# First MLP product of a hybrid encoder block turned token-major, with a seven-product scheme for a quarter of its K pairs

## The chip, the cores and the metric

The kernel runs on one core of one Trainium2 chip. The metric is the device time of one execution, in microseconds (us). A second number, the span of the profiled execution, runs from its first instruction to its last. Engines are called as in the profile: PE is TensorE's matmuls, PEld its weight loads, DVE is VectorE, ACT is ScalarE, POOL is GpSimd, and SP is the engine that only issues DMAs here.

## The reference

One layer of a streaming encoder on 256 tokens with model width 2048, in float32. `n = RMSNorm(h)`, an input projection, two groups of heads (gated DeltaNet and HGRN2), an output projection, and then a squared-ReLU MLP:

```
h = h + concat(y_A, y_B) @ W_out
n = rms_norm(h, norm_ffn_w)
h = h + square(relu(n @ w1)) @ w2        # w1: 2048 x 8192, w2: 8192 x 2048
out = rms_norm(h, norm_final_w)
```

The change touches `n @ w1` and what stands next to it. The RMS factor of a token's row commutes with ReLU and with the squaring, so the kernel leaves it out of `n` and multiplies the row by its square (`fs[:, 6 + hf]`, line 765) only after `@ w2`.

## The kernel before, in words

**Precision.** The matmuls take a rounded float32 form (`F32R`). To keep float32 accuracy each operand is split in two, `hi` (rounded, by ACT, line 117) and `lo = w - hi` (by DVE, line 118), and a product is `hi*hi + lo*hi + hi*lo`, three matmuls into one accumulator. Weights arrive as float32 tiles of 128 x 2048 (1 MB, one DMA on SP's queue, three buffers) and are split in pieces of 128 x 1024, with three buffers for `hi` and three for `lo`.

**Stages, in order of time.** The input projection with the heads' own work between (to 447 us); the output projection (447 to 550 us, lines 652 to 679); the first MLP product (550 to 913 us, lines 698 to 715); the second MLP product (913 us to the end, lines 718 to 756) with the final norm.

**Output projection (line 664).** Token-major: the stationary operand is 128 x 128 of y transposed (`yT`), the moving operand 128 x 512 of the split weight. The sum goes to `h`, 128 tokens to a half, two halves (`hf`). After each half of the columns, `h` is transposed by PE in 128 x 128 blocks (line 678) into `hT`, which ACT and DVE scale by the norm weight and split (`to_T`, lines 164 to 167).

**First MLP product.** Feature-major: the stationary operand is a 128 x 128 block of the weight, the moving one is `hT`. Line 709 takes `hi` of the weight against 512 columns (256 tokens of `hi`, 256 of `lo`), line 710 `lo` of the weight against the 256 `hi` tokens. For each of 64 blocks of 128 features and each of 16 K blocks there is one such pair, 1024 pairs in all. Four feature blocks share four PSUM banks (`acc` or `accb`, in turn). Lines 713 to 715 add the two halves of a bank and write `relu(x)*x`, feature-major, into `g`.

**Second MLP product (`ff2`, line 731).** Token-major: stationary is 128 x 128 of the split `g` (`gs`), moving 128 x 512 of the split weight. Three matmuls for each of 64 K blocks, two token halves and four groups of 512 columns, 1536 in all (the last of them in two halves of 256 columns).

**Order of work.** The program is written in the order above, and a planner that simulates the engines orders each engine's queue: what is ready goes first, and an instruction's place in the source is its priority. The two transposes at a time that stand between matmuls of the next half in the profile come from that. On the chip each queue keeps the planned order.

Of the kernel before, what the change touches and what calls it, by code (L numbers as in the profile page):

```python
# [73 lines left out]
def hybrid_block(ctx: ExitStack, tc: tile.TileContext, x, xt, w_in, w_ab, params, w_out, w_ff1, w_ff2,  # L74
                 norm_final_w, consts, out):
    nc = tc.nc
    PE, ACT, DVE, POOL, SP = nc.tensor, nc.scalar, nc.vector, nc.gpsimd, nc.sync
# [24 lines left out]
    def acc_a():  # L102
        return psA.tile([P, 512], F32, tag="acc", name="acc")
# [37 lines left out]
    for a, b in zip(xs, ws):  # L141
        SP.dma_start(*a)
        SP.dma_start(*b)
    SP.dma_start(cst, consts)
    wab = mp.tile([P, KT, 16], F32, tag="Xt", name="wab")
    SP.dma_start(wab, w_ab)

    def C(name):
        a, b = _CONST_COLS[name]
        return cst[:, a:b]  # L150

    ident, ones = C("ident"), C("ones")
    eps = C("eps")
# [487 lines left out]
    def acc_b():  # L641
        return psB.tile([P, 512], F32, tag="accb", name="accb")

    hT = bpool.tile([P, KT, 2 * T], F32R, tag="xT", name="hT")
    h = bpool.tile([P, 2 * D], F32, tag="h", name="h").rearrange("p (f c) -> p f c", f=2)
# [5 lines left out]
    fs = cpool.tile([P, 16], F32, tag="fs", name="fs")  # L651
    for nh in range(2):
        accs = [acc_a() for _ in range(4)]
        for kp in range(8):
            w = wtile()
            SP.dma_start(w, w_out[nh * 8 + kp])
            for kk in range(2):
                k = 2 * kp + kk
                hi, lo = split(w[:, kk * 1024:(kk + 1) * 1024], 1024)
                for hf in range(2):  # L660
                    for a, ww in ((0, hi), (T, hi), (0, lo)):
                        st = yT(k, a + hf * P, a + hf * P + P)
                        for c in range(2):
                            PE.matmul(accs[2 * hf + c], lhsT=st, rhs=ww[:, c * 512:(c + 1) * 512],  # L664
                                      start=(k == 0 and a == 0 and ww is hi), stop=(k == 2 * NH - 1 and ww is lo))
        for hf in range(2):
            for c in range(2):
                hv = h[:, hf, nh * 1024 + c * 512:nh * 1024 + (c + 1) * 512]
                DVE.tensor_tensor(out=hv, in0=accs[2 * hf + c], in1=hv, op=ALU.add)
            hv = h[:, hf, nh * 1024:(nh + 1) * 1024]  # L670
            ACT.activation(sqj, hv, AF.Square, accum_out=fs[:, 2 * hf + nh:2 * hf + nh + 1])
        for k2 in range(4):
            pt = acc_b()
            for kk in range(2):
                k = nh * 8 + k2 * 2 + kk
                ptk = pt[:, kk * T:(kk + 1) * T]
                for hf in range(2):
                    PE.transpose(ptk[:, hf * P:(hf + 1) * P], h[:, hf, k * P:(k + 1) * P], ident)
                to_T(hT, k, ptk, cols[:, 16 + k:17 + k])
    for hf in range(2):  # L680
        DVE.tensor_tensor(out=fs[:, 4 + hf:5 + hf], in0=fs[:, 2 * hf:2 * hf + 1], in1=fs[:, 2 * hf + 1:2 * hf + 2],
                          op=ALU.add)
# [11 lines left out]
    def g(f):
        return gt[f // NG][:, f % NG, :]

    nfw = fp.tile([P, D], F32, tag="nfw", name="nfw")
    for fg in range(NF // 4):
        accs = [acc_a() if fg % 2 == 0 else acc_b() for _ in range(4)]
        for kq in range(4):  # L700
            w = wtile()
            SP.dma_start(w, w_ff1[fg * 4 + kq])
            for q in range(2):
                hi, lo = split(w[:, q * 1024:(q + 1) * 1024], 1024)
                for kk in range(2):
                    k = 4 * kq + 2 * q + kk
                    for f in range(4):
                        cs = slice(kk * 512 + f * P, kk * 512 + (f + 1) * P)
                        PE.matmul(accs[f], lhsT=hi[:, cs], rhs=hT[:, k, :], start=(k == 0), stop=False)  # L709
                        PE.matmul(accs[f][:, T:], lhsT=lo[:, cs], rhs=hT[:, k, 0:T], start=False, stop=(k == KT - 1))  # L710
        for f in range(4):
            lot = fp.tile([P, T], F32, tag="lotf", name="lotf", bufs=2)
            ACT.copy(lot, accs[f][:, T:])
            DVE.tensor_tensor(out=lot, in0=accs[f][:, 0:T], in1=lot, op=ALU.add)
            DVE.scalar_tensor_tensor(out=g(4 * fg + f), in0=lot, scalar=0.0, in1=lot, op0=ALU.max, op1=ALU.mult)
    SP.dma_start(nfw, norm_final_w.unsqueeze(0).to_broadcast([P, D]))

    accs = [[acc_a() for _ in range(4)], [acc_b() for _ in range(4)]]
    TAIL = 3
    held = []  # L720

# [10 lines left out]
                      start=(first and a == 0 and ww is hi), stop=(last and ww is lo))  # L732

    keep = None
    for f in range(NF):
        w = wtile()
        SP.dma_start(w, w_ff2[f])
        gs = fp.tile([P, 2 * T], F32R, tag="gs", name="gs", bufs=4)
        split(g(f), None, gs[:, 0:T], gs[:, T:])
        n = f - (NF - TAIL)  # L740
        if n == 0:
            keep = fp.tile([P, TAIL - 1, 2, D], F32R, tag="g0", name="keep")
        hl = []
# [13 lines left out]
    fin = fp.tile([P, 12], F32, tag="fin", name="fin")  # L757
    sqf = fp.tile([P, 512], F32, tag="sqf", name="sqf")
    o = fp.tile([P, 2, D], F32, tag="o", name="o", bufs=1)
    NP = 5  # L760
    DVE.memset(fin, 0.0)

    def piece(hf, n, a, b, acc):
        hv = h[:, hf, a:b]
        DVE.scalar_tensor_tensor(out=hv, in0=acc, scalar=fs[:, 6 + hf:7 + hf], in1=hv, op0=ALU.mult, op1=ALU.add)
        ACT.activation(sqf[:, 0:b - a], hv, AF.Square, accum_out=fin[:, hf * NP + n:hf * NP + n + 1])
        DVE.scalar_tensor_tensor(out=o[:, hf, a:b], in0=hv, scalar=float(D) ** 0.5, in1=nfw[:, a:b], op0=ALU.mult,
                                 op1=ALU.mult)

    def row_rstd(hf, n, last):  # L770
# [11 lines left out]

    def scaled(hf, eng, a, b, s):
        if eng is ACT:
            ACT.activation(h[:, hf, a:b], o[:, hf, a:b], AF.Copy, scale=s)
        else:
            DVE.tensor_scalar(h[:, hf, a:b], o[:, hf, a:b], s, None, ALU.mult)
        (ACT if eng is ACT else SP).dma_start(out[0, hf * P:(hf + 1) * P, a:b], h[:, hf, a:b])

    hv = h[:, 1, 1536:2048]  # L790
# [27 lines left out]
def _laid_out(i):  # L818
# [5 lines left out]
    for base in (0, 4112):  # L824
        v = w[:, base:base + 4096].reshape(2, 8, P, 2, 2, NH, P)
        groups.append(v.transpose(5, 3, 0, 2, 1, 4, 6).reshape(4 * NH, P, 2048))

    def columns(a):
        return a.reshape(-1, P).T

# [9 lines left out]
        "w_ff1": i["w_ff1"][0].reshape(4, 4, P, 16, 512).transpose(3, 0, 2, 1, 4).reshape(64, P, 2048),  # L840
# [24 lines left out]
```

## Time and profile before

| | |
|---|---|
| median of 3 runs (range) | 1270.77 us (1270.59 to 1271.01) |
| the profiled execution's own time | 1271.04 us |
| its span | 1269.3 us |
| PE busy | 1239.6 us, 98% of the span |
| DVE busy | 855.0 us, 67% |
| ACT busy | 673.9 us, 53% |
| DMA | 229.65 MB, mean 181 GB/s |

A row of the timeline has the start in us, the time from the first start to the last end, engine, line, operation, output <- inputs, shapes and count, and in brackets the idle time before it. Matmuls overlap, so a row's duration is not what a matmul costs: the distance from start to start is. A row of the windows has the stretch, its length, and for each engine its busy time and its instructions. A row of the groups has the count, the busy time, the mean duration in ns, then the idle time before such instructions and what ended it.

### The profile page before, as it was taken

The page shows a single profiled execution, that of the slowest core. Times are in us where ns is not written, and L with a number is a line of the kernel's source. Part 1 is how long each engine was busy: PE and PEld are TensorE (multiplying, and loading weights), DVE is VectorE, ACT ScalarE, POOL GpSimd, SP SyncE. Part 2 cuts the span into 40 slices and gives each one's busy share as a digit, 9 for nine tenths or more (in the row PEclk, how much of TensorE's full clock was granted, in tenths as well). Part 3 has the DMA queues.
Part 4 walks back from the last instruction along what each step waited for, and adds up shares of the span by engine and source line. Part 5 has one row for each costly group of instructions (what it writes and reads, how often), then busy time and mean ns, then how long its engine had stood idle before and what let it go on. Part 6 is the DMA issues. An engine that isn't in the chain of part 4 may idle for free.

```text
span 1269.3 us, 18524 instructions
## 1 busy us (share of the span) xinstructions
PE 1239.6 (98%) x7293; PEld 1050.3 (83%) x7293; DVE 855.0 (67%) x1211; ACT 673.9 (53%) x973; POOL 166.3 (13%) x216
## 2 busy tenths in 40 slices
PE   7999999998999999999999999999999999999997
PEld 5888888876788887888888888888888888888886
DVE  7789999889988996566555565555655545545556
ACT  7567677655667775455444444444444444444453
POOL 1233433278300130000000000000000000000000
PEclk9999999998999999999999999999999999999999
DMA  8455555533434544465555545555455555555552
GB/s 314 147 176 172 179 186 187 173 141 133 151 104 174 189 167 166 168 222 177 197 181 184 199 170 195 189 178 196 168 201 195 199 199 190 187 191 195 199 201 97
DMA packets 35798, 229.65 MB, mean 181 GB/s; under 512 B 4536, under 2 KB 5440, under 8 KB 8960
## 3 DMA queue, kind: packets, MB, share of 16 engines
q1 hardware_dynamic: 33408, 225.63, 50.4%
q0 software_dynamic: 1728, 2.11, 1.3%
q8 instruction: 57, 0.93, 0.3%
q10 hardware_dynamic: 576, 0.74, 0.2%
q14 instruction: 29, 0.24, 0.1%
HBM read 225.83 MB, written 2.63 MB: 180 GB/s over the span
## 4 chain that ended last, share of the span: by engine, by line
issue 62%; PE 30%; POOL 3%; DVE 2%; DMA 2%; ACT 0%; SPq 0%; POOLq 0%; ACTq 0%; DVEq 0%
PE acc L286 15%; PE acc L287 8%; PE acc L664 3%; POOL Xt L424 1%; POOL X L426 1%; DMA big<-in_xt_dram 1%; DMA w<-in_w_in_dram 1%; DVE E L568 1%; PE pk L368 1%; DVE E L553 0%; DVE lo L118 0%; PE pd L583 0%; PE pab L221 0%; PE po L507 0%; PE pk L369 0%
## 5 line engine op out<-in xcount | busy, mean ns | idle before, releaser
L118 DVE TENSOR_TENSOR lo<-w,hi 128x1024 fp32r<-128x1024 f32 (+1 forms) x416 | 517.3, 1244 | 363.5 <-ACT hi L117 362.4
L117 ACT CAST hi<-w 128x1024 fp32r<-128x1024 f32 (+1 forms) x416 | 433.2, 1042 | 442.0 <-PE accb L731 177.1
L286 PE MATMUL acc<-xT,hi 128*128 128x512 f32 x1024 | 363.3, 401 | 7.1 <-ACT hi L117 6.7
L287 PE MATMUL acc<-xT,lo 128*128 128x256 f32 x1024 | 283.9, 286 | 6.2 <-DVE lo L118 6.2
L286 PEld LDWEIGHTS acc<-xT,hi 128*128 128x128 f32 x1024 | 191.6, 191 | 47.3 <-ACT hi L117 7.3
L287 PEld LDWEIGHTS acc<-xT,lo 128*128 128x128 f32 x1024 | 194.9, 191 | 15.0 <-DVE lo L118 10.5
L709 PE MATMUL acc<-hT,hi 128*128 128x512 f32 x512 | 181.3, 399 | 0.0
L709 PE MATMUL accb<-hT,hi 128*128 128x512 f32 x512 | 180.8, 398 | 0.0
L731 PE MATMUL accb<-hi,gs 128*128 128x512 f32 x494 | 170.0, 389 | 0.0
L710 PE MATMUL accb<-hT,lo 128*128 128x256 f32 x512 | 143.2, 281 | 0.0
L710 PE MATMUL acc<-hT,lo 128*128 128x256 f32 x512 | 142.8, 281 | 0.0
L731 PE MATMUL acc<-hi,gs 128*128 128x512 f32 (+1 forms) x500 | 134.2, 388 | 0.0
L709 PEld LDWEIGHTS accb<-hT,hi 128*128 128x128 f32 x512 | 96.1, 188 | 23.9
L709 PEld LDWEIGHTS acc<-hT,hi 128*128 128x128 f32 x512 | 96.0, 188 | 23.4
L731 PEld LDWEIGHTS acc<-hi,gs 128*128 128x128 f32 x500 | 93.7, 188 | 19.3
L731 PEld LDWEIGHTS accb<-hi,gs 128*128 128x128 f32 x494 | 92.7, 188 | 19.3
L779 POOL TENSOR_TENSOR fin<-fin,cst 128x1 f32<-128x1 f32 x2 | 1.1, 564 | 773.9 <-issue 766.5
L710 PEld LDWEIGHTS acc<-hT,lo 128*128 128x128 f32 x512 | 96.5, 189 | 0.2
L710 PEld LDWEIGHTS accb<-hT,lo 128*128 128x128 f32 x512 | 96.6, 189 | 0.1
L731 PE MATMUL accb<-lo,gs 128*128 128x512 f32 x247 | 95.4, 389 | 0.0
L731 PE MATMUL acc<-lo,gs 128*128 128x512 f32 (+1 forms) x250 | 77.7, 388 | 0.0
L731 PEld LDWEIGHTS acc<-lo,gs 128*128 128x128 f32 x250 | 46.9, 188 | 9.7
(251 smaller groups left out, 1250.1 us busy)
## 6 DMA issues: line engine op xcount, KB each, us to landing
w<-in_w_ff_dram SPq DMA_DIRECT2D x128, 1024.0 KB, 4.9
w<-in_w_in_dram SPq DMA_DIRECT2D x62, 1024.0 KB, 4.9
w<-in_w_out_dram SPq DMA_DIRECT2D x16, 1024.0 KB, 4.9
big<-in_xt_dram SPq DMA_DIRECT2D x8, 256.0 KB, 6.2
w<-in_w_in_dram SPq DMA_DIRECT2D x8, 256.0 KB, 6.3
h<-in_x_dram SPq DMA_DIRECT2D x2, 1024.0 KB, 9.2
dt<-scr_g POOLq DMA_DIRECT2D x8, 128.0 KB, 5.6
nfw<-in_norm_final_w_dram SPq DMA_DIRECT2D x1, 1024.0 KB, 4.7
```

The costliest lines, as they stand in the source:

```text
L117: ACT.copy(hi, w)
L118: eng.tensor_tensor(out=lo, in0=w, in1=hi.bitcast(F32), op=ALU.subtract)
L286: PE.matmul(accs[g], lhsT=hi[:, kk, g, :], rhs=xT[:, k, :], start=(k == 0), stop=False)
L287: PE.matmul(accs[g][:, T:], lhsT=lo[:, kk, g, :], rhs=xT[:, k, 0:T], start=False, stop=(k == KT - 1))
L368: PE.matmul(pk0, lhsT=R[:, 1, 0:P], rhs=qk.rearrange("p a t -> p (a t)"), start=True, stop=True)
L424: POOL.tensor_tensor(out=t3, in0=X[:, j, j + 1:].unsqueeze(2).to_broadcast([np_, nr, ncol]), in1=X[:, j, 0:ncol].unsqueeze(1).to_broadcast ...
L426: POOL.tensor_tensor(out=X[:, j + 1:, 0:ncol], in0=X[:, j + 1:, 0:ncol], in1=t3, op=ALU.subtract)
L568: DVE.tensor_tensor(out=ev, in0=ev, in1=view(gx, 0, [[2 * m, nb], [T + m, 2], [1, m]]), op=ALU.mult)
L664: PE.matmul(accs[2 * hf + c], lhsT=st, rhs=ww[:, c * 512:(c + 1) * 512], start=(k == 0 and a == 0 and ww is hi), stop=(k == 2 * NH - 1 and ...
L709: PE.matmul(accs[f], lhsT=hi[:, cs], rhs=hT[:, k, :], start=(k == 0), stop=False)
L710: PE.matmul(accs[f][:, T:], lhsT=lo[:, cs], rhs=hT[:, k, 0:T], start=False, stop=(k == KT - 1))
L731: PE.matmul(dst, lhsT=gs[:, a + hf * P:a + hf * P + P], rhs=ww[:, at:at + n], start=(first and a == 0 and ww is hi), stop=(last and ww is lo))
```

## The change

The first MLP product is made token-major: stationary are 128 x 128 blocks of the transposed `h`, moving are 128 x 512 of the split weight, and the result is 128 tokens by 512 features. The weight is laid out anew on the host: a tile holds two K blocks by 2 x 512 features, as a 2 x 2 block matrix B. There are eight groups of 1024 features (`ng`) and eight K pairs in each (`kp`). For six K pairs the 2 x 2 x 2 = 8 block products are made as they are, with three matmuls each (`plain_quad`). For K pairs 2 and 5 (`SUMS`) seven products of sums of blocks are made (Strassen's scheme in Winograd's form), three of them into the plain accumulators E and four into a second set of banks M. DVE forms the sums of the weight's blocks (`T1`, `T2`, `T4`) ahead of their split; the sums of h's blocks are formed once (`blocks`). After K pair 5 DVE combines the four M banks into `C4`; at the end of a group it adds E, ACT takes the ReLU, and then PE transposes the 128 x 512 pieces back (`turn`, 16 blocks to a group), ACT squaring them out of PSUM into `g`. E and M change places with each group between `acc` and `accb`.

What goes with it: `h` is no longer kept but written to DRAM (`scr_h`) and read again at the start of the second product; a second, right-hand pool gives `hi` and `lo` two more buffers each, five in turn (`split_pair`); the constants that only the first stage needs move to a pool that is freed (`NKEEP`), which with `fin` in the constants' pool makes left-hand and right-hand tiles start at equal remainders of 512 bytes; the turns of the last group, and the blocks of the second half of `h`, are run as `fills` between matmuls; the second product's first two K blocks take the two column halves one after the other, since the last group's banks come free late.

```
+    def split_pair(w):
+        n = pairs[0] = pairs[0] + 1
+        pool, t = (spool, "") if n % 5 < 3 else (wp2, "2")
+        return split(w, None, *[pool.tile([P, 1024], F32R, tag=p + t, name=p + t) for p in ("hi", "lo")])
...
+    KP = KT // 2
+    SUMS = (2, 5)
+    sets = bpool.tile([P, 8192], F32R, tag="xT", name="sets")
+    sets2 = tp.tile([P, 1792], F32R, tag="s2", name="sets2")
...
     for nh in range(2):
-        accs = [acc_a() for _ in range(4)]
+        acc = (acc_a, acc_b)[nh]
+        accs = [acc() for _ in range(4)]
...
+            SP.dma_start(scr_h[hf, :, nh * 1024:(nh + 1) * 1024], hv)
+        for kp in range(nh * 4, nh * 4 + 4):
+            if nh == 0:
+                blocks(kp, acc)
+            else:
+                fills.append(lambda kp=kp: blocks(kp, acc_b))
...
+    def product(dst, a, b, start, stop):
+        (ah, al), (bh, bl) = a, b
+        PE.matmul(dst, lhsT=ah, rhs=bh, start=start, stop=False)
+        PE.matmul(dst, lhsT=al, rhs=bh, start=False, stop=False)
+        PE.matmul(dst, lhsT=ah, rhs=bl, start=False, stop=stop)
...
+    def turn(ng, n, src, acc):
+        half, hf = n // 2, n % 2
+        pt = acc()
+        for c in range(4):
+            PE.transpose(pt[:, c * P:(c + 1) * P], src[:, c * P:(c + 1) * P], ident)
+        ACT.activation(g(8 * ng + 4 * half, 4)[:, :, hf * P:(hf + 1) * P], pt.rearrange("p (c t) -> p c t", c=4),
+                       AF.Square)
+    def plain_quad(E, st, B, first, last, n_fill):
+        def one(n, kk):
+            hf, c = divmod(n, 2)
+            a = [st[:, kk, s + hf * P:s + hf * P + P] for s in (0, T)]
+            product(E[n], a, B[kk][c], first and kk == 0, last and kk == 1)
+        for n, kk in [(n, kk) for n in range(4) for kk in range(2)] if last else \
+                [(n, kk) for kk in range(2) for n in range(4)]:
+            one(n, kk)
+            if (n, kk) == (3, 0):
+                fill(n_fill)
+    for ng in range(NGR):
+        bank_e, bank_m = (acc_a, acc_b) if ng % 2 == 0 else (acc_b, acc_a)
+        E = [bank_e() for _ in range(4)]
+        M = None
+        for kp in range(KP):
             w = wtile()
-            SP.dma_start(w, w_ff1[fg * 4 + kq])
...
-                        PE.matmul(accs[f], lhsT=hi[:, cs], rhs=hT[:, k, :], start=(k == 0), stop=False)
-                        PE.matmul(accs[f][:, T:], lhsT=lo[:, cs], rhs=hT[:, k, 0:T], start=False, stop=(k == KT - 1))
...
+            SP.dma_start(w, w_ff1[ng * KP + kp])
+            if kp not in SUMS:
+                B12, B11 = halves(split_pair(w[:, 0:1024]))
+                B21, B22 = halves(split_pair(w[:, 1024:2048]))
+                plain_quad(E, a_plain(kp), ((B11, B12), (B21, B22)), kp == 0, kp == KP - 1, 0 if kp == 0 else 2)
...
+                continue
+            if M is None:
+                M = [bank_m() for _ in range(4)]
+            TT = tp.tile([P, 2048], F32, tag="TT", name="TT")
+            B = [w[:, c * 512:(c + 1) * 512] for c in range(4)]
+            T1, T2, T4 = [TT[:, c * 512:(c + 1) * 512] for c in (0, 2, 3)]
+            B21, B22 = halves(split_pair(w[:, 1024:2048]))
+            DVE.tensor_tensor(out=TT[:, 0:1024].rearrange("p (a c) -> p a c", a=2), in0=view(w, 0, [[1536, 2], [1, 512]]),
+                              in1=view(w, 512, [[-512, 2], [1, 512]]), op=ALU.subtract)
+            B1, B3 = halves(split_pair(TT[:, 0:1024]))
+            DVE.tensor_tensor(out=T2, in0=B[3], in1=T1, op=ALU.subtract)
+            DVE.tensor_tensor(out=T4, in0=B[2], in1=T2, op=ALU.subtract)
+            B2, B4 = halves(split_pair(TT[:, 1024:2048]))
+            B11 = [tp.tile([P, 512], F32R, tag=t, name=t) for t in ("hi4", "lo4")]
+            split(B[1], None, *B11)
...
+            for dst, a, b in ((E[0], 1, B21), (E[1], 6, B22), (p5, 3, B1), (p7, 5, B3), (p6, 4, B2), (E[2], 2, B4),
+                              (p1, 0, B11)):
+                m = a in (0, 3, 4, 5)
+                product(dst, A[a], b, a0 and m, z0 and m)
+            if z0:
+                C4 = cp.tile([P, 4, 512], F32, tag="C", name="C4")
+                ACT.copy(C4[:, 0], p1)
...
+        for at, p in ((0, E[0]), (2, E[1]), (1, E[2]), (3, E[3])):
+            DVE.tensor_tensor(out=C4[:, at], in0=p, in1=C4[:, at], op=ALU.add)
+            ACT.activation(C4[:, at], C4[:, at], AF.Relu)
+            fills.append(lambda ng=ng, at=at, src=C4[:, at], acc=bank_e: turn(ng, at, src, acc))
+    t1.close()
...
+    tail = bpool.tile([P, 8192], F32, tag="xT", name="tail")
+    h, nfw, o0 = tail[:, 0:2 * D].rearrange("p (f c) -> p f c", f=2), tail[:, 2 * D:3 * D], tail[:, 3 * D:]
+    for hf in range(2):
+        SP.dma_start(h[:, hf, :], scr_h[hf])
     SP.dma_start(nfw, norm_final_w.unsqueeze(0).to_broadcast([P, D]))
...
+        if f < 2:
+            hl = [split_pair(w[:, 0:1024]), None]
+            for hf in range(2):
+                for c in range(2):
+                    ff2(f, hf, c, gs, hl)
+                    fill(f == 0 and hf == 1)
+            fill(2)
+            late.append((f, gs, w))
```

More of the change, by code (lines that the diff above doesn't have):

```diff
@@ L149, in C @@
         a, b = _CONST_COLS[name]
-        return cst[:, a:b]
+        return cst[:, a:b] if b <= NKEEP else cst_a[:, a - NKEEP:b - NKEEP]
     ident, ones = C("ident"), C("ones")
@@ L642, in acc_b, with a_plain, a_sums @@
         return psB.tile([P, 512], F32, tag="accb", name="accb")
-    hT = bpool.tile([P, KT, 2 * T], F32R, tag="xT", name="hT")
-    h = bpool.tile([P, 2 * D], F32, tag="h", name="h").rearrange("p (f c) -> p f c", f=2)
+    wp2 = ctx.enter_context(tc.tile_pool(name="wp2", bufs=2, side="right"))
+    t1 = ExitStack()
+    tp = t1.enter_context(tc.tile_pool(name="tp", bufs=1, side="right"))
+    pairs = [0]
+    def split_pair(w):
[6 more added lines that the diff above has]
+    sets2 = tp.tile([P, 1792], F32R, tag="s2", name="sets2")
+    plain = [kp for kp in range(KP) if kp not in SUMS]
+    def a_plain(kp):
+        n = plain.index(kp)
+        return sets[:, n * 1024:(n + 1) * 1024].rearrange("p (k s) -> p k s", k=2)
+    def a_sums(kp):
+        t, at = (sets, 6144) if kp == SUMS[0] else (sets2, 0)
+        return t[:, at:at + 1792].rearrange("p (s n t) -> p s n t", s=2, n=7)
+    h = hpool.tile([P, 2 * D], F32, tag="h", name="h").rearrange("p (f c) -> p f c", f=2)
+    scr_h = dpool.tile([2, P, D], F32, tag="scr_h", name="scr_h")
     for hf in range(2):
@@ L651, in hybrid_block, with fill, blocks @@
     fs = cpool.tile([P, 16], F32, tag="fs", name="fs")
+    fills = []
+    def fill(n=1):
+        for _ in range(n):
+            if fills:
+                fills.pop(0)()
+    def blocks(kp, acc):
+        pt = acc()
+        for kk in range(2):
+            for hf in range(2):
+                c = (2 * kp + kk) * P
+                PE.transpose(pt[:, kk * T + hf * P:kk * T + hf * P + P], h[:, hf, c:c + P], ident)
+        wc = [cols[:, 16 + 2 * kp + kk:17 + 2 * kp + kk] for kk in range(2)]
+        if kp in plain:
+            for kk in range(2):
+                to_T(a_plain(kp), kk, pt[:, kk * T:(kk + 1) * T], wc[kk])
+            return
+        X = op.tile([P, 8, P], F32, tag="X", name="X", bufs=2)
+        ACT.activation(view(X, P, [[-P, 2], [1, P]]), pt[:, 0:T].rearrange("p (a t) -> p a t", a=2), AF.Copy, scale=wc[0])
+        ACT.activation(X[:, 2:4, :].rearrange("p a t -> p (a t)"), pt[:, T:2 * T], AF.Copy, scale=wc[1])
+        DVE.tensor_tensor(out=X[:, 4], in0=X[:, 0], in1=X[:, 3], op=ALU.add)
+        DVE.tensor_tensor(out=X[:, 5], in0=X[:, 4], in1=X[:, 1], op=ALU.subtract)
+        DVE.tensor_tensor(out=X[:, 6], in0=X[:, 1], in1=X[:, 0], op=ALU.subtract)
+        DVE.tensor_tensor(out=X[:, 7], in0=X[:, 2], in1=X[:, 5], op=ALU.subtract)
+        st = a_sums(kp)
+        split(X[:, 1:8], None, st[:, 0], st[:, 1])
     for nh in range(2):
-        accs = [acc_a() for _ in range(4)]
+        acc = (acc_a, acc_b)[nh]
+        accs = [acc() for _ in range(4)]
         for kp in range(8):
@@ L658, in hybrid_block @@
                 k = 2 * kp + kk
-                hi, lo = split(w[:, kk * 1024:(kk + 1) * 1024], 1024)
+                wk = w[:, kk * 1024:(kk + 1) * 1024]
+                hi, lo = split(wk, 1024) if nh == 0 else split_pair(wk)
                 for hf in range(2):
@@ L671, in hybrid_block @@
             ACT.activation(sqj, hv, AF.Square, accum_out=fs[:, 2 * hf + nh:2 * hf + nh + 1])
[L672 to L682, printed above, removed]
@@ L694, in g @@
[L694 to L700, printed above, removed]
-            w = wtile()
-            SP.dma_start(w, w_ff1[fg * 4 + kq])
[L703 to L715, printed above, removed]
@@ new lines, in halves @@
+    def halves(hl):
+        return [[t[:, c * 512:(c + 1) * 512] for t in hl] for c in range(2)]
+    def turn(ng, n, src, acc):
+        half, hf = n // 2, n % 2
+        pt = acc()
+        for c in range(4):
[12 more added lines that the diff above has]
+                fill(n_fill)
@@ new lines, in hybrid_block, with columns @@
+    t1.close()
+    f2 = ctx.enter_context(tc.tile_pool(name="f2", bufs=1, side="right"))
+    tail = bpool.tile([P, 8192], F32, tag="xT", name="tail")
+    h, nfw, o0 = tail[:, 0:2 * D].rearrange("p (f c) -> p f c", f=2), tail[:, 2 * D:3 * D], tail[:, 3 * D:]
+    for hf in range(2):
+        SP.dma_start(h[:, hf, :], scr_h[hf])
+    SP.dma_start(nfw, norm_final_w.unsqueeze(0).to_broadcast([P, D]))
+    accs = [[None] * 4, [None] * 4]
+    def columns(q, bank):
+        for hf in range(2):
+            for c in (2 * q, 2 * q + 1):
+                accs[hf][c] = bank()
@@ L719, in hybrid_block @@
+    columns(0, bank_m)
     TAIL = 3
@@ L734, in hybrid_block @@
     keep = None
+    late = []
     for f in range(NF):
@@ L742, in hybrid_block @@
             keep = fp.tile([P, TAIL - 1, 2, D], F32R, tag="g0", name="keep")
+        if f < 2:
+            hl = [split_pair(w[:, 0:1024]), None]
+            for hf in range(2):
+                for c in range(2):
+                    ff2(f, hf, c, gs, hl)
+                    fill(f == 0 and hf == 1)
+            fill(2)
+            late.append((f, gs, w))
+            if f == 1:
+                columns(1, bank_e)
+                c1.close()
+                for f_, gs_, w_ in late:
+                    hl = [None, split_pair(w_[:, 1024:2048])]
+                    for hf in range(2):
+                        for c in (2, 3):
+                            ff2(f_, hf, c, gs_, hl)
+            continue
         hl = []
@@ L766, in piece @@
         ACT.activation(sqf[:, 0:b - a], hv, AF.Square, accum_out=fin[:, hf * NP + n:hf * NP + n + 1])
-        DVE.scalar_tensor_tensor(out=o[:, hf, a:b], in0=hv, scalar=float(D) ** 0.5, in1=nfw[:, a:b], op0=ALU.mult,
+        DVE.scalar_tensor_tensor(out=o[hf][:, a:b], in0=hv, scalar=float(D) ** 0.5, in1=nfw[:, a:b], op0=ALU.mult,
                                  op1=ALU.mult)
@@ L803, in hybrid_block @@
     for n in range(2):
-        bank = acc_a()[:, 0:256]
+        bank = bank_m()[:, 0:256]
         for f, gs, hl in held:
```

61 lines of the change are left out of this document (42 added, 19 removed).

## Prediction

> **What bounds the kernel now.** The first part of the page, busy time and share of each engine, says who is at the limit:
>
> ```profile
> PE 1239.6 (98%) x7293; PEld 1050.3 (83%) x7293; DVE 855.0 (67%) x1211; ACT 673.9 (53%) x973; POOL 166.3 (13%) x216
> ```
>
> A share is an average, so next I read the windows, one for each stage of the MLP:
>
> ```profile
> core 0: us, PE busy (x) PEld busy (x) DVE busy (x) ACT busy (x) POOL busy (x), PEclk, DMA share, GB/s
> 549.70:912.60 362.90, 362.90 (x2064) 314.88 (x2064) 205.12 (x270) 160.28 (x206) 0.00 (x0) 1.00 0.54 189
> 560.50:912.60 352.10, 352.10 (x1998) 305.43 (x1997) 196.92 (x253) 151.97 (x192) 0.00 (x0) 1.00 0.53 188
> 912.60:1244.00 331.40, 331.40 (x1464) 274.44 (x1463) 175.92 (x194) 151.15 (x188) 0.00 (x0) 1.00 0.55 194
> ```
>
> In the first product (first two rows) and in the second (third row) PE has no gap at all, at full clock; DVE is at 57%, ACT at 44%, the DMA engines at about half. So only PE's own instructions count there, and the view by groups tells which they are, and who waits for whom:
>
> ```profile
> L709 PE MATMUL acc<-hT,hi 128*128 128x512 f32 x512 | 181.3, 399 | 0.0
> L709 PE MATMUL accb<-hT,hi 128*128 128x512 f32 x512 | 180.8, 398 | 0.0
> L710 PE MATMUL acc<-hT,lo 128*128 128x256 f32 x512 | 142.8, 281 | 0.0
> L710 PE MATMUL accb<-hT,lo 128*128 128x256 f32 x512 | 143.2, 281 | 0.0
> ```
>
> ```profile
> ACT hi L117 <- PE accb L731: 177.1, 118, 2.4
> ACT hi L117 <- PE acc L709: 92.1, 62, 1.8
> ```
>
> The last column of the groups is idle time before such matmuls: nothing. It is the split (line 117) that waits for PE to free a buffer, not the reverse.
>
> **What a matmul costs.** Records overlap, so I divide stretches without a gap by their counts. First product: 352.10 us over 1998 matmuls, 999 pairs of 512 and 256 columns: 0.3525 us a pair, 0.459 ns a column. Second product: 331.40 over 1464 matmuls of 512 columns: 0.2264 us each, 0.442 ns a column. So the short matmul is dearer by the column than the long. The input projection, with the same pairs, shows how much of that is the form:
>
> ```profile
> 99.88 0.39 PE L286 MATMUL acc<-xT,hi 128*128 128x512 f32 x1
> ...
> 100.23 0.39 PE L286 MATMUL acc<-xT,hi 128*128 128x512 f32 x1
> ...
> 101.96 0.39 PE L286 MATMUL acc<-xT,hi 128*128 128x512 f32 x1
> ```
>
> Six pairs lie between the first and the last start, 2.08 us, 0.347 us a pair. If a matmul costs a constant and an amount by the column, 0.2264 for 512 and 0.347 for 768 in two give 0.413 ns a column and 15 ns a matmul; the first product's pair has 6 ns more that this doesn't explain.
>
> **The change part by part.**
>
> *Matmuls removed:* 1024 pairs x 0.3525 = 361.0 us. With the 16 transposes of line 678 that fall into the stage this makes its 362.9.
>
> *Matmuls added:* in a group six plain K pairs of 8 x 3 and two of 7 x 3, so 186, in eight groups 1488, all of 512 columns. Their form (three matmuls into one bank, stationary hi, lo, hi, moving hi, hi, lo of the weight) is `ff2`'s, line 731, so I take that row: 1488 x 0.2264 = 336.9 us. From above it is bounded by the column rate of the stage they replace, 512 x 0.459 = 235 ns; from below by 0.2264, since the output projection has the same form at the same distance:
>
> ```profile
> 512.34 0.61 PE L664 MATMUL acc<-hi,yTa 128*128 128x512 f32 x2
> 512.79 0.62 PE L664 MATMUL acc<-lo,yTa 128*128 128x512 f32 x2
> 513.25 1.03 PE L678 MATMUL accb<-cst,h 128*128 128x128 f32 x8
> 514.04 1.87 PE L664 MATMUL acc<-hi,yTa 128*128 128x512 f32 x7
> 515.75 0.62 PE L664 MATMUL acc<-lo,yTa 128*128 128x512 f32 x2
> 516.21 0.39 PE L664 MATMUL acc<-hi,yTa 128*128 128x512 f32 x1
> ```
>
> *Transposes added:* 8 groups x 16 = 128, of 128 x 128. The same rows price them: from 513.25 to 516.21 lie 8 transposes and 9 matmuls; 2.96 - 9 x 0.2264 = 0.92 us, 0.115 us each, the disturbance of the matmuls behind them included. 128 x 0.115 = 14.7 us, all on PE. The 32 of line 678 stay (`blocks`). As a group, line 678 looks dearer:
>
> ```profile
> L678 PE MATMUL accb<-cst,h 128*128 128x128 f32 x32 | 5.6, 274 | 0.0
> ```
>
> Its mean record is 274 ns long, yet eight of them lie in 1.03 us: the length is latency, of which the next transpose doesn't wait for the end. I take the distance, 0.115; below it I allow a tenth, and its upper bound is each alone, 0.274 (fourth rival).
>
> *Sum of PE:* -361.0 + 336.9 + 14.7 = -9.4 us. Apart: the form alone (1536 plain matmuls, 347.7 us) would bring 13.3, the scheme's 48 spared matmuls bring 10.9, and the transposes take 14.7 back.
>
> *The splits and sums on DVE and ACT*, off PE's path as long as they keep ahead. The rows:
>
> ```profile
> L118 DVE TENSOR_TENSOR lo<-w,hi 128x1024 fp32r<-128x1024 f32 x408 | 511.8, 1255 | 362.7 <-ACT hi L117 361.5 <-PE accb L678 0.6
> L118 DVE TENSOR_TENSOR lo<-w,hi 128x512 fp32r<-128x512 f32 x8 | 5.5, 688 | 0.9 <-ACT hi L117 0.9
> L177 DVE TENSOR_TENSOR sums<-sums,junk 128x1024 f32<-128x1024 f32 x3 | 3.7, 1224 | 0.2 <-ACT junk L175 0.2
> L669 DVE TENSOR_TENSOR h<-acc,h 128x512 f32<-128x512 f32 x8 | 5.0, 683 | 1.5 <-PE acc L664 1.5
> L117 ACT CAST hi<-w 128x1024 fp32r<-128x1024 f32 x408 | 428.4, 1051 | 442.0 <-PE accb L731 177.1 <-PE accb L709 95.2 <-PE acc L709 92.1
> L117 ACT CAST hi<-w 128x512 fp32r<-128x512 f32 x8 | 4.8, 604 | 0.0
> L766 ACT ACTIVATE sqf<-h 128x512 f32<-128x512 f32 x7 | 4.4, 630 | 10.8 <-DVE h L765 10.8
> ```
>
> A plain K pair: DVE 2 x 1.255 = 2.5, ACT 2.1, PE 24 x 0.2264 = 5.4 us. A summed one: DVE 3 x 1.255 + 0.688 of split, 1.224 + 2 x 0.683 of sums, 7.0 us; ACT 3.8; PE 21 x 0.2264 = 4.75. So there DVE is slower than PE by 2.3 us. The five buffers cover it: when PE starts the plain pair before, two hold its pieces, and the summed pair's three pieces find a buffer that is free, one freed 2.7 us ago and one freed now. Even if DVE began all its work only then, with ACT's first cast it is done 1.05 + 7.0 = 8.1 us later, and PE wants the third piece at 5.4 + 4 x 0.68 = 8.15 us. In a group DVE has 18 x 1.255 + 2 x 0.688 + 2 x (1.224 + 1.366) + 8 x 0.683 = 34.6 us, ACT 18 x 1.051 + 2 x 0.604 + 9 x 0.630 = 25.8, and PE 186 x 0.2264 + 16 x 0.115 = 43.9. I cost it at nothing; at worst it is the second rival.
>
> *The end of a group:* E's banks are finished one by one, 6 matmuls (1.36 us) apart; behind the last come DVE's add (0.683) and ACT's ReLU (0.63), and the turns of PE are queued 24 matmuls (5.4 us) into the next group, whose banks were emptied after K pair 5. Nothing is late: 0. Queued behind a turn that waited would be all of PE. In the second product's start the turns come after 12 matmuls, 2.7 us against 1.3: 0.
>
> *`h` to DRAM and back:* four writes of 0.5 MB wait on SP for line 669, two reads of 1 MB wait there for the last matmul that reads `sets`, and the weight loads are queued behind. The rows for such traffic:
>
> ```profile
> w<-in_w_ff_dram SPq DMA_DIRECT2D x128, 1024.0 KB, 4.9
> h<-in_x_dram SPq DMA_DIRECT2D x2, 1024.0 KB, 9.2
> nfw<-in_norm_final_w_dram SPq DMA_DIRECT2D x1, 1024.0 KB, 4.7
> ```
>
> At the start of the second product three weight tiles are loaded, PE work for 3 x 5.4 = 16.3 us. The fourth must land 2.3 us (cast and subtraction) before that, at 14 us; behind two reads in 9.2, `norm_final_w` in 4.7 and its own 4.9, one after the other, it would land at 18.8, 5 us late. But those times overlap, as the two 9.2 show (a tile alone takes 4.9), so I take 0 and keep 0 to 5.
>
> *The constants' split in two loads, the moved tiles, the remainders:* before, weights and `hT` are allocated at one remainder too; no row shows another; 0, and what it could cost lies within the matmul's bounds.
>
> The profiled execution took 1271.04 us, 1.7 outside its span, and lies 0.3 above the median; 1271.04 - 9.4 = 1261.6, or 1261.4 beside the median. I say 1261.6.
>
> **Rivals.**
>
> 1. *The column rate of the stage stays.* If what makes the first product dearer by the column is not the short matmul but the place (four banks in turn, tiles, what else reads), a new matmul takes 235 ns: 1488 x 0.0086 = 12.8 us more, 1274.4, slower. It decides from 9.4 / 1488 = 6.3 ns a matmul on, at 232.7 ns. For it: the 6 ns a pair that the constant doesn't explain. Against: the input projection's pairs and two stages of the new form. Chance 0.10. The Trainium skill ("TensorE: Matmul & The Clock Gate", Part 2, back-to-back issue gap) has N / 2.4 + 2.5 ns for a matmul, nearly a pure column rate: by it the pairs are 332.8 us and the new matmuls 321.1, and with the transposes the change loses 3 us. The trace has 226 ns where this gives 216, and 352 where it gives 325, so it bears the rule out in neither case.
>
> 2. *DVE becomes the bound.* If the lead of five pieces is lost, each summed pair holds PE up by 2.3 us, 16 x 2.3 = 36 us, 1298; 0.6 us each cancels the gain. For it: 7.0 against 4.75 us. Against: 79% over the group, and the waits above, where ACT waits for PE. Chance 0.06.
>
> 3. *Small new waits* (a turn, an add queued ahead of a split, the read of `h`): up to 9 us, 1262 to 1270; half of them would be 1266. Chance 0.16, half of it below 1268.2.
>
> 4. *Each transpose at its record's length.* If a turn's four transposes stood one behind the other at 0.274 us, they would cost 128 x (0.274 - 0.115) = 20.4 us more: 1282, slower; it decides from 0.188 us a transpose on. For it: groups of four from a freshly written source into a freshly emptied bank, which the trace doesn't show. Against: the eight in 1.03 us. Chance 0.03. The Trainium skill ("TensorE: Matmul & The Clock Gate", Part 4) gives about 275 ns for a PE transpose within a kernel; by it the 128 would take 35 us and the change would lose 11. The trace agrees with the record's length and not with the distance.
>
> That the change doesn't do what it says can't be: the counts are in the code.
>
> **How the numbers follow.** My forecast has 0.65. Its own range, 0.2264 to 0.2275 us a matmul (1.6 us) and a tenth either way on a transpose (1.5 us), is 1260 to 1264.5. With rivals 1 and 3 taken in, 1259 to 1274.5 leaves out rivals 2 and 4 and a little below. 0.2% is 2.5 us, about what a measurement of this kernel can tell from none: faster is below 1268.2 (0.65 + 0.08 = 0.73), the same up to 1273.3 (0.08), slower 0.10 + 0.06 + 0.03 = 0.19.
>
> **What would show it.** Stage of the first product about 353.5 us, 1488 matmuls of 512 columns at 226 ns from start to start, 128 more transposes in fours that cost 0.45 to 0.5 us, PE without idle time, ACT's casts still waiting for PE. Wrong: distances of 232 ns and more (rival 1); PE idle with DVE's `lo` as the releaser in K pairs 2 and 5 (rival 2); PE idle at each group's start or in the first 20 us of the second product (rival 3).

## The result, and the profile after

| | before | after |
|---|---|---|
| median (range), six runs each, side by side | 1271.52 us (1270.59 to 1272.93) | 1261.23 us (1260.94 to 1263.17) |
| ratio, 95% interval | | 0.9922 (0.9909 to 0.9934) |
| the profiled execution, its span | 1271.04, 1269.3 | 1261.03, 1259.3 |

The change makes the kernel faster by 0.8%; 1261.6 us was forecast. In the runs below one execution, of the run with the remainder shifted by 128 bytes, had a granted clock of 0.515 in place of 0.987 to 0.996 and took 2407.84 us; its ratio leaves that execution out. First the page, then the stages as windows, with columns as before:

```profile
PE 1229.4 (98%) x6861; PEld 1029.9 (82%) x6861; DVE 915.7 (73%) x1233; ACT 716.2 (57%) x1015; POOL 166.9 (13%) x216
```

```profile
503.00:548.67 45.67, 45.67 (x211) 37.95 (x210) 31.97 (x39) 24.11 (x32) 0.00 (x0) 1.00 0.62 218
548.67:900.25 351.58, 351.58 (x1618) 292.64 (x1616) 263.90 (x288) 198.92 (x242) 0.00 (x0) 1.00 0.54 193
900.25:1243.00 342.75, 342.75 (x1522) 284.04 (x1521) 179.47 (x196) 154.30 (x197) 0.00 (x0) 1.00 0.56 195
```

The second row is the first product from its first matmul to its end: 351.58 us without a gap on PE, where it was 362.9. DVE has 59 us more to do in it and still has a quarter of the time left. The groups of the new stage, three matmuls of a product (lines 753 to 755) and the turn's transposes, for one of the two sets of banks each:

```profile
L753 PE MATMUL accb<-hi,sets 128*128 128x512 f32 x248 | 97.2, 392 | 0.0
L754 PE MATMUL accb<-hi,sets 128*128 128x512 f32 x248 | 96.6, 389 | 0.0
L755 PE MATMUL accb<-lo,sets 128*128 128x512 f32 x248 | 96.6, 390 | 0.0
L765 PE MATMUL accb<-cst,C 128*128 128x128 f32 x64 | 8.4, 272 | 0.0
```

No idle time stands before any of them. The waits of the stage (who waited for whom, us in total, times, longest), without the first row, in which DVE waits for ACT:

```profile
ACT hi L119 <- PE accb L754: 49.3, 52, 1.9
ACT hi L119 <- PE acc L754: 46.4, 49, 1.9
ACT hi L119 <- issue: 25.3, 15, 1.9
ACT C L843 <- DVE C L842: 16.4, 8, 2.2
ACT hi L119 <- DMA w<-in_w_ff_dram: 13.4, 8, 2.8
```

It is still mostly the split that waits for PE. New are waits of ACT for DVE's adds at a group's end and for weights that have not landed; none of them reaches PE. And the timeline at the end of the second group's first K pair, where two turns follow on each other:

```profile
597.38 0.39 PE L753 MATMUL accb<-hi,sets 128*128 128x512 f32 x1
597.61 0.39 PE L754 MATMUL accb<-hi,sets 128*128 128x512 f32 x1
597.83 0.39 PE L755 MATMUL accb<-lo,sets 128*128 128x512 f32 x1
598.07 1.03 PE L765 MATMUL acc<-cst,C 128*128 128x128 f32 x8
598.86 0.48 PE L753 MATMUL accb<-hi,sets 128*128 128x512 f32 x1
...
599.86 0.39 PE L754 MATMUL accb<-hi,sets 128*128 128x512 f32 x1
```

Matmuls start 0.227 us apart. From 598.07 to 599.86 lie eight transposes and four matmuls (three of the rows between are left out): 1.79 - 4 x 0.2264 = 0.88 us, 0.11 us a transpose.

The span is 10.0 us shorter. 1.05 us of it come before the first product: its first matmul starts at 548.67 in place of 549.72, PE waiting once for 2.0 us in the output projection, at 500 us, where it waited 2.9. The first product gains 11.4, the second has the last group's turns in it and gives 1.8 back, the end 0.6. In the profiles of the runs below the time ahead of the first product varies by almost 3 us (it starts at 548.2 to 551), though PE's work up to there is the same. So I compare stages where a microsecond matters.

### The profile page after: what moved, and what is told of

It reads as the page before. It is cut to its first block, busy times and chain, and to the rows that moved or that the text cites. A ratio compares the mean times of both kernels' runs of the same rounds, so it can differ in the third digit from the quotient of the medians.

```text
span 1259.3 us, 17732 instructions
## 1 busy us (share of the span) xinstructions
PE 1229.4 (98%) x6861; PEld 1029.9 (82%) x6861; DVE 915.7 (73%) x1233; ACT 716.2 (57%) x1015; POOL 166.9 (13%) x216
## 4 chain that ended last, share of the span: by engine, by line
PE 91%; POOL 3%; DVE 2%; issue 2%; ACT 1%; DMA 0%; SPq 0%; POOLq 0%; DVEq 0%; ACTq 0%
PE acc L290 16%; PE acc L873 14%; PE accb L873 14%; PE acc L291 8%; PE acc L755 4%; PE accb L754 4%; PE acc L754 4%; PE accb L755 4%; PE accb L753 4%; PE acc L753 4%; PE accb L727 3%; PE acc L727 3%; POOL Xt L428 1%; POOL X L430 1%; PE acc L765 1%
## 5 line engine op out<-in xcount | busy, mean ns | idle before, releaser
L120 DVE TENSOR_TENSOR lo<-w,hi 128x1024 fp32r<-128x1024 f32 (+1 forms) x416 | 505.5, 1221 | 248.5 <-ACT hi L119 242.5
L291 PEld LDWEIGHTS acc<-xT,lo 128*128 128x128 f32 x1024 | 194.9, 191 | 15.8 <-DVE lo L120 11.4
L873 PE MATMUL acc<-hi,gs 128*128 128x512 f32 (+1 forms) x500 | 153.8, 389 | 0.0
L873 PE MATMUL accb<-hi,gs 128*128 128x512 f32 x494 | 151.8, 389 | 0.0
L753 PE MATMUL accb<-hi,sets 128*128 128x512 f32 x248 | 97.2, 392 | 0.0
L753 PE MATMUL acc<-hi,sets 128*128 128x512 f32 x248 | 97.2, 392 | 0.0
L873 PE MATMUL acc<-lo,gs 128*128 128x512 f32 (+1 forms) x250 | 97.2, 389 | 0.0
L755 PE MATMUL accb<-lo,sets 128*128 128x512 f32 x248 | 96.6, 390 | 0.0
L754 PE MATMUL acc<-hi,sets 128*128 128x512 f32 x248 | 96.6, 389 | 0.0
L754 PE MATMUL accb<-hi,sets 128*128 128x512 f32 x248 | 96.6, 389 | 0.0
L755 PE MATMUL acc<-lo,sets 128*128 128x512 f32 x248 | 96.3, 390 | 0.0
L120 DVE TENSOR_TENSOR lo<-TT,hi 128x1024 fp32r<-128x1024 f32 x32 | 39.1, 1224 | 36.0 <-ACT hi L119 34.2
L119 ACT CAST hi<-TT 128x1024 fp32r<-128x1024 f32 x32 | 33.5, 1048 | 37.7 <-issue 13.1
```

The lines of the kernel that those rows point to most:

```text
L119: ACT.copy(hi, w)
L120: eng.tensor_tensor(out=lo, in0=w, in1=hi.bitcast(F32), op=ALU.subtract)
L291: PE.matmul(accs[g][:, T:], lhsT=lo[:, kk, g, :], rhs=xT[:, k, 0:T], start=False, stop=(k == KT - 1))
L753: PE.matmul(dst, lhsT=ah, rhs=bh, start=start, stop=False)
L754: PE.matmul(dst, lhsT=al, rhs=bh, start=False, stop=False)
L755: PE.matmul(dst, lhsT=ah, rhs=bl, start=False, stop=stop)
```

## The experiments

The theory: PE's instructions alone set the time, at the prices of the prediction; what DVE, ACT and the DMA queue get on top is covered. The rival in most runs: some of the cover (banks, buffers, DVE) is thin, and costs or saves time that the sum doesn't hold. Ratios are to the kernel before, timed beside each run.

**The form without the scheme.**

```
-    SUMS = (2, 5)
+    SUMS = ()
...
-            DVE.tensor_tensor(out=C4[:, at], in0=p, in1=C4[:, at], op=ALU.add)
-            ACT.activation(C4[:, at], C4[:, at], AF.Relu)
+            ACT.activation(C4[:, at], p, AF.Relu)
```

> The changed kernel without the seven-product scheme: all eight K pairs plain, 1536 matmuls in the first product; E alone goes through ReLU, turns and squaring, no second bank set. My theory: 48 matmuls more than with the scheme, 48 x 0.2264 = 10.9 us, so 1272.1 us against the changed kernel's 1261.2, and no gain over the kernel before (form +13.3, transposes -14.7). Rival: the scheme's sums, the second bank set and the combination of M cost PE time that the profile hides; then leaving them out gives some of the 10.9 back, under 1270 us.

Measured: 1272.27 us, ratio 0.9998 (0.9989 to 1.0007). The first product as a window:

```profile
549.03:911.48 362.45, 362.45 (x1666) 301.53 (x1664) 161.97 (x146) 170.67 (x203) 0.00 (x0) 1.00 0.55 188
```

362.45 - 351.58 = 10.87 us for 48 matmuls, 0.2265 each. The scheme's sums, its second set of banks and its combination cost PE nothing, and the form alone is worth nothing: what the long matmuls bring, the turns take back.

**One set of banks for each.**

```
-        bank_e, bank_m = (acc_a, acc_b) if ng % 2 == 0 else (acc_b, acc_a)
+        bank_e, bank_m = acc_a, acc_b
...
-            fills.append(lambda ng=ng, at=at, src=C4[:, at], acc=bank_e: turn(ng, at, src, acc))
+            fills.append(lambda ng=ng, at=at, src=C4[:, at], acc=bank_m: turn(ng, at, src, acc))
...
-    columns(0, bank_m)
+    columns(0, bank_e)
...
-                columns(1, bank_e)
+                columns(1, bank_m)
```

> The changed kernel with E always in acc and M always in accb; the turns then use accb, the second product's first column half acc. My theory: a group's banks are finished 1.36 us apart and emptied 0.68 us later, and the next group wants them at 0, 0.68, 1.36 and 2.04 us, so PE waits little: at most 1 us a group where a subtraction of 1.2 us stands ahead of an add, 1261 to 1265 us. Rival: the change of banks is what keeps PE busy at the group's end; without it each of seven boundaries shows 1.5 to 3 us, 1272 to 1282 us.

Measured: 1263.12 us, ratio 0.9923 (0.9911 to 0.9936), first product 352.23 us, 0.65 more for seven boundaries. The rival's 1.5 to 3 us for each are not there. The change of banks is worth next to nothing. That a group's last K pair finishes its banks one after the other would explain it; no run changes that order.

**Three buffers.**

```
-        n = pairs[0] = pairs[0] + 1
-        pool, t = (spool, "") if n % 5 < 3 else (wp2, "2")
-        return split(w, None, *[pool.tile([P, 1024], F32R, tag=p + t, name=p + t) for p in ("hi", "lo")])
+        return split(w, 1024)
```

> The changed kernel with three buffers for hi and lo in place of five. My theory (a lead of pieces covers the 2.3 us by which DVE is slower than PE in a summed pair): with three, counted by hand, the second summed piece is ready 5.0 us after the start of the plain pair before and wanted at 6.8, the third 7.7 against 8.15, the next pair's first 9.65 against 10.2: just in time, 1261 to 1266 us. Rival: the lead is lost, each of 16 summed pairs holds PE up by about 2.3 us, 1290 us and more.

Measured: 1263.15 us, ratio 0.9923 (0.9910 to 0.9935), first product 351.32 us. With two summed pairs of eight even three buffers are lead enough; the prediction named five as the cover, and fewer do.

**Three summed pairs.** `SUMS = (2, 4, 6)`, with one more tile for the sums of `h`.

> The changed kernel with three K pairs summed (2, 4, 6) in place of two: 24 matmuls fewer, one more set of h's sums. My theory (PE alone counts as long as DVE keeps its lead): -24 x 0.2264 = -5.4 us, 1255.8 us, with PE without idle time; DVE has 39 us of work in a group, PE 43.3. Rival: DVE's 7.0 us in a summed pair already bound it there, then PE waits for lo in K pairs 4 and 6 and the time is 1261 us or more.

Measured: 1256.40 us, ratio 0.9881 (0.9867 to 0.9894).

```profile
548.82:895.54 346.72, 346.72 (x1594) 287.72 (x1592) 296.69 (x329) 213.01 (x257) 0.00 (x0) 1.00 0.57 197
```

4.9 us less than with two, where 5.4 were counted, PE without a gap, DVE at 86% of the stage. This version beats both kernels.

**Four summed pairs.** `SUMS = (2, 3, 5, 6)`.

> The changed kernel with four K pairs summed (2, 3, 5, 6): 48 matmuls fewer. In a group DVE has 4 x 2.5 + 4 x 7.04 + 5.5 = 43.7 us, PE 180 x 0.2264 + 1.8 = 42.6. If DVE could be spread over the whole group: 1261.2 - 10.9 + 8 = about 1258 us at best. Since two summed pairs stand side by side (14.1 us of DVE against 9.5 of PE) I expect PE to wait for lo there, 1258 to 1275 us; at 1250 DVE wouldn't be the bound, and my price of its work would be wrong.

Measured: 1259.86 us, ratio 0.9907 (0.9893 to 0.9920). Window, waits of the weight loads and of ACT, and a stretch of PE's timeline:

```profile
548.39:896.54 348.15, 345.57 (x1570) 281.80 (x1568) 317.82 (x360) 218.67 (x271) 0.00 (x0) 1.00 0.56 194
```

```profile
PEld acc L754 <- ACT hi L119: 5.2, 9, 1.2
PEld accb L754 <- ACT hi L119: 3.9, 9, 0.6
```

```profile
ACT hi L119 <- DVE TT L818: 25.1, 11, 3.7
...
ACT hi L119 <- DVE TT L822: 13.7, 14, 2.5
```

```profile
691.00 0.48 PE L754 MATMUL accb<-hi,sets 128*128 128x512 f32 x1
691.31 0.40 PE L755 MATMUL accb<-hi,sets 128*128 128x512 f32 x1
691.83 0.51 PE L754 MATMUL accb<-hi,sets 128*128 128x512 f32 x1
```

At the prices of the prediction the stage would be 1440 x 0.2264 + 128 x 0.115 = 340.7 us (the same sum gives 351.6 for the changed kernel); it takes 7.4 more. PE waits for ACT's `hi`, and ACT for DVE's sums (lines 818 and 822): 691.31 to 691.83 is 0.52 us for a matmul of 0.227. So DVE's work reaches PE from the fourth pair on, though PE waited for `hi` of the sums and not for `lo`, as I had put it. But it isn't more than PE's over a group, as 43.7 against 42.6 us had said. Those 43.7 us add up the lengths of records, and DVE's records overlap too:

```profile
675.66 1.23 DVE L120 TENSOR_TENSOR lo<-TT,hi 128x1024 fp32r<-128x1024 f32 x1 [1.11 <-ACT hi L119]
676.80 1.22 DVE L120 TENSOR_TENSOR lo<-w,hi 128x1024 fp32r<-128x1024 f32 x1
```

The starts are 1.14 us apart. DVE was busy for 317.82 us of the stage, 39.7 us a group, or 91%. It falls behind for a time and has idle time at others: of the 15 us before the wait at 691.83 it was busy for 14.7, of the 15 before another at 675.68 for 12.2. That two summed pairs stand side by side fits this, but no run has four that stand apart.

**Sums on POOL.** Four pairs, and the first of the three subtractions moved; in the second of these runs `TT` also has two buffers.

```
-            DVE.tensor_tensor(out=TT[:, 0:1024].rearrange("p (a c) -> p a c", a=2), in0=view(w, 0, [[1536, 2], [1, 512]]),
+            POOL.tensor_tensor(out=TT[:, 0:1024].rearrange("p (a c) -> p a c", a=2), in0=view(w, 0, [[1536, 2], [1, 512]]),
```

> Four summed K pairs (2, 3, 5, 6) with the subtraction of 128 x 1024 for T1 and T3 on POOL in place of DVE. DVE then has 4 x 2.5 + 4 x 5.8 + 5.5 = 38.8 us in a group against PE's 42.6; POOL about 4.4 us for each (two of its 128 x 512 at 2.24). My theory (DVE's work bound the run with four pairs): the waits of PE go and the time is about 1261.2 - 10.9 = 1250.3 us, up to 1254 as POOL's result comes 3 us later than DVE's. Rival: POOL's reads hold DVE's two-input operations up, or its latency stands in the chain of the summed pairs, and the time stays at 1257 us or more.

> As the run with four pairs and POOL, with two buffers for the sums TT, so that POOL can form the next pair's sums while the last ones are split. If the latency of the sums is what is left over there, this takes it away: 1250 to 1251.5 us. If the other run is there already, or DVE is held up by POOL, no difference within 1 us.

Measured: 1288.09 us, ratio 1.0122 (1.0106 to 1.0139), and 1290.02, 1.0138 (1.0124 to 1.0152). My theory failed, the second buffer brought nothing, and the rival's first half held. DVE's groups in the first product, with four pairs and then with POOL:

```profile
L120 DVE TENSOR_TENSOR lo<-w,hi 128x1024 fp32r<-128x1024 f32 x94 | 114.2, 1221 | 5.6 <-ACT hi L119 4.5 <-PE acc L756 0.6 <-PE accb L756 0.4
L120 DVE TENSOR_TENSOR lo<-w,hi 128x512 fp32r<-128x512 f32 x31 | 21.3, 689 | 9.9 <-PE accb L756 5.0 <-PE acc L756 5.0
```

```profile
L120 DVE TENSOR_TENSOR lo<-w,hi 128x1024 fp32r<-128x1024 f32 x95 | 146.7, 1554 | 16.4 <-ACT hi L119 16.3
L120 DVE TENSOR_TENSOR lo<-w,hi 128x512 fp32r<-128x512 f32 x31 | 36.5, 1178 | 0.0
```

The mean subtraction from `w` is longer, 1554 and 1178 ns in place of 1221 and 689, and DVE is busier than before it was relieved (332 us in the stage against 318). The Trainium skill ("SBUF — State Buffer", "SBUF: two separate sides") states that a DVE operation with two SBUF inputs and a GpSimd operation that reads SBUF exclude each other for a whole instruction. The trace agrees, and shows that the wait lies inside the record:

```profile
595.20 2.62 POOL L818 TENSOR_TENSOR TT<-w 128x1024 f32<-128x1024 f32 x1 [14.54 <-DMA w<-in_w_ff_dram]
595.50 0.68 DVE L837 TENSOR_TENSOR C<-accb,C 128x512 f32<-128x512 f32 x1
596.20 2.71 DVE L120 TENSOR_TENSOR lo<-w,hi 128x1024 fp32r<-128x1024 f32 x1
```

POOL's subtraction ends at 597.82, and DVE's, begun at 596.20, at 598.91, 1.09 us later. The add at 595.50, which reads one input from PSUM, keeps its 0.68 us beside POOL, and so do the two others that begin while a subtraction of POOL runs. Of the 126 subtractions of line 120 from `w` in the stage 23 begin while POOL's runs. Each of them is drawn out like this and ends 1.1 us (128 x 1024) or 0.55 us (128 x 512) after it; together they last some 47 us longer than at 1221 and 689 ns. How much of the 375 us that the stage took comes from this and how much from weight tiles that POOL holds longer isn't separated.

**The remainders.** One number is changed, the length of the constants' tile, by 8, 16, 32 and 64 columns (its load keeps the old length):

```
-    cst = cpool.tile([P, NKEEP], F32, tag="cst", name="cst")
+    cst = cpool.tile([P, NKEEP + 8], F32, tag="cst", name="cst")
```

> The changed kernel with the constants' tile 256 bytes longer: left-hand tiles start at remainder 224 of 512 bytes, right-hand ones stay at 480, nothing else changes. A: the remainder doesn't matter to PE, 1261.2 us within 1.5, matmuls at 226 ns in all three stages. B: unequal remainders of stationary and moving operand slow the matmuls that mix both sides (about two fifths of the first product, three fifths of the second, none of the input projection): up to the 235 ns of the old first product, some 1500 x 8 ns = 12 us, about 1273 us. I hold A at 0.5.

> The changed kernel with the constants' tile 32 bytes longer: left-hand tiles at remainder 0 of 512 bytes, right-hand ones at 480. A (no effect of remainders): 1261.2 us within 1.5. B (unequal remainders slow the matmuls that mix both sides): the same sign as with 256 bytes, some us more than 1261.2.

> The changed kernel with the constants' tile 64 bytes longer: left-hand tiles start at remainder 32 of 512 bytes, right-hand ones at 480, so both at 32 of 64. With 32 bytes more the matmuls that mix both sides took 233 ns in place of 227 and the kernel 1273.9 us; with 256 more nothing changed. If what counts is the remainder of 64 bytes: nothing, 1261 to 1263 us, 227 ns. If it is that of 128 or of 256 bytes: slower as with 32, about 1273 us.

> The changed kernel with the constants' tile 128 bytes longer: left-hand tiles at remainder 96 of 512 bytes, right-hand ones at 480, so 128 apart; 32 and 64 bytes apart took 1273.9 and 1271.1 us, 256 apart 1262.9. If the remainder of 128 bytes counts: 1261 to 1263 us, 227 ns for matmuls that mix both sides. If that of 256: slower, 1270 us or more, 229 to 234 ns for those.

Measured, with the mean distance of some 2900 matmuls of 512 columns in the two products, parted by whether the moving operand and the next stationary one lie on the same side:

| shift, bytes | median us | ratio (95%) | first product us | same side ns | mixed ns |
|---|---|---|---|---|---|
| 32 | 1273.89 | 1.0015 (1.0006 to 1.0024) | 356.56 | 228.0 | 233.4 |
| 64 | 1271.11 | 0.9986 (0.9977 to 0.9995) | 356.37 | 228.3 | 230.8 |
| 128 | 1274.01 | 1.0009 (1.0000 to 1.0018) | 356.65 | 228.1 | 232.9 |
| 256 | 1262.86 | 0.9917 (0.9904 to 0.9931) | 351.57 | 226.7 | 226.7 |

Without a shift both distances are 226.7. With 64 bytes the direction counts too: with the moving operand on the right and the stationary one on the left (first product) the mean is 233, the other way round (second product) 229.

The run with 32 bytes shows the effect within one stage. In its second product the stationary operand is always on the right; at 1003.44 the moving one passes from a right-hand buffer to a left-hand one:

```profile
1001.40 0.62 PE L873 MATMUL accb<-hi,gs 128*128 128x512 f32 x2
1001.85 0.39 PE L873 MATMUL accb<-lo,gs 128*128 128x512 f32 x1
1002.08 0.62 PE L873 MATMUL accb<-hi,gs 128*128 128x512 f32 x2
...
1002.76 0.62 PE L873 MATMUL accb<-hi,gs 128*128 128x512 f32 x2
1003.21 0.39 PE L873 MATMUL accb<-lo,gs 128*128 128x512 f32 x1
1003.44 0.63 PE L873 MATMUL acc<-hi,gs 128*128 128x512 f32 x2
1003.90 0.40 PE L873 MATMUL acc<-lo,gs 128*128 128x512 f32 x1
1004.14 0.63 PE L873 MATMUL acc<-hi,gs 128*128 128x512 f32 x2
1004.61 0.40 PE L873 MATMUL acc<-lo,gs 128*128 128x512 f32 x1
1004.84 0.63 PE L873 MATMUL acc<-hi,gs 128*128 128x512 f32 x2
```

Three matmuls take 0.68 us up to there and 0.70 from there on. I had held no effect at even chances; it is there, and of the shifts tried only 256 bytes is free of it. So the remainder of 256 bytes counts, not that of 512, and 32 bytes of it cost more than the whole change brings. The mechanism behind it isn't shown by these runs.

**Why the old form was dear.** The kernel before, four long matmuls and then four short ones in place of pairs:

```
                     for f in range(4):
...
                         PE.matmul(accs[f], lhsT=hi[:, cs], rhs=hT[:, k, :], start=(k == 0), stop=False)
+                    for f in range(4):
+                        cs = slice(kk * 512 + f * P, kk * 512 + (f + 1) * P)
                         PE.matmul(accs[f][:, T:], lhsT=lo[:, cs], rhs=hT[:, k, 0:T], start=False, stop=(k == KT - 1))
```

> The kernel before with the order of its first product changed: for each K block the four matmuls of 512 columns (hi), then the four of 256 columns (lo), in place of pairs. C: a matmul costs a constant and an amount by the column; the order doesn't matter, 1271 us within 2. D: the short matmul is held by its weight load, whose record is 188 ns long: four short ones in a row then cost up to 188 ns each in place of about 117, 1024 x 0.07 = 72 us, up to 1343 us, and alternating with long ones hides that. Which it is says why the old form was dear.

Measured: 1270.69 us, ratio 0.9987 (0.9978 to 0.9996).

```profile
699.81 0.63 PE L712 MATMUL acc<-hT,lo 128*128 128x256 f32 x4
700.28 1.09 PE L709 MATMUL acc<-hT,hi 128*128 128x512 f32 x4
701.21 0.64 PE L712 MATMUL acc<-hT,lo 128*128 128x256 f32 x4
```

Four short ones start within 0.47 us, 0.117 each, though each has a weight load with a record of 189 ns: the load is no bound. Four long ones take 0.93 us, 0.232 each, still more than the 0.227 of the other form. A constant for each matmul fits the order's small effect; these 0.232, and the 6 ns by which this stage's pairs are dearer than the input projection's, are not explained, and no run tests whether the place of the operands has a part in them.

## Why the prediction was right, point by point

- *Matmuls added*: 0.2264 us each was taken from the second product's row. The three stages with 1536, 1488 and 1464 of them differ by 10.9 and 4.9 us for 10.9 and 5.4 counted, so the price and the count carry the sum. The column rate (first rival, 235 ns) is out: 227 ns in the timeline.
- *Transposes*: 0.115 us taken, 0.11 measured; the fourth rival's 0.274 is out, the records still last 272 ns.
- *Splits and sums at nothing*: right, and with more cover than the argument claimed: three buffers are enough, and a third summed pair too. The second rival shows itself with the fourth pair. DVE's price was too high, though: 34.6 us a group were added up from the lengths of records, which for PE's transposes had been refused with good reason. DVE was busy for 263.90 us of the stage, 33.0 a group, with what was left of the sums of `h` in it.
- *The end of a group, the second product's start, `h` through DRAM at nothing*: right. No PE wait stands at a boundary, and `h` coming back from DRAM took 5.9 us a tile with no wait of PE for the weights queued behind it:

```profile
scr_h<-h SPq DMA_DIRECT2D x4, 512.0 KB, 6.2
tail<-scr_h SPq DMA_DIRECT2D x2, 1024.0 KB, 5.9
tail<-in_norm_final_w_dram SPq DMA_DIRECT2D x1, 1024.0 KB, 9.0
```

- *The remainders at nothing*: right only because both sides do have the same remainder. As an edit it was weighed wrongly: I said what it could cost lay within the matmul's bounds, but I had no mechanism for it and gave it no rival; unequal by 32, 64 or 128 bytes, it takes all or nearly all of the gain (ratios 0.9986 to 1.0015). What the first rival held in general, that the place of the operands bears on a matmul's price, is thus true of this kernel; it didn't come about because the places were made equal.
- *The sum*: -9.4 us forecast; -10.0 in the profiled executions, 1.05 of it before the first product, which no step of mine moved. The steps' own share is -9.6 in the two products and +0.6 at the end, which the sum doesn't hold either; that these two and the 1.05 so nearly cancel is luck. The 353.5 us that the prediction gave for the stage were 1.9 too many: it put all 128 new transposes there, but the last group's 16 run in the second product, which takes 1.8 longer.

## What to carry to other kernels

A stage on a full PE is priced by counting its matmuls and multiplying with a start-to-start distance from a stage of the same form; a change of form that needs transposes has to pay for them first, and here only the matmuls that a seven-product scheme spares remained. Such a scheme is bought with VectorE time, so sum DVE's work for a group against PE's, by its starts and not by the lengths of records: here it pays up to 86% of DVE's stage and stops at 91%. When a kernel allocates tiles from both ends of SBUF, make stationary and moving operands start at the same remainder of 256 bytes.

## What the runs showed of the hardware that was not expected

- A matmul of 512 columns takes 227 ns when both operands start at the same remainder of 256 bytes, and 231 to 233 on average when they are 32, 64 or 128 bytes apart. The Trainium skill ("TensorE: Matmul & The Clock Gate", Part 2) states that weights are loaded through a read port of their own and take no read bandwidth from the running matmul; these runs show that the place of the one operand does bear on the time of the other.
- Subtractions of DVE on 128 x 1024 start 1.14 us apart where their records last 1.22, so a sum of records overstates DVE's work.
- A short matmul of 256 columns starts 0.117 us after the last one even four in a row, with weight loads of 189 ns in the records.
- A subtraction of DVE begun beside one of POOL, all inputs in SBUF, ended 1.1 us (128 x 1024) or 0.55 us (128 x 512) after POOL's, while three adds with one input in PSUM kept their 0.68 us. The means grew from 1221 to 1554 ns and from 689 to 1178 ns, so that work moved to an idle POOL made DVE busier, not freer.
